# A two-layer hybrid diffusion trunk on one core: more room for row tasks, a second buffer of squares, and half of one pair's weight splits on VectorE

## The chip, the cores and the metric

The kernel runs on one core of one Trainium2 chip. The core has TensorE (PE in the profile; PEld is its weight load), VectorE (DVE), ScalarE (ACT), GpSimd (POOL) and SyncE (SP), which issues the transfers. The metric is the device time of one execution in microseconds; a kernel's time is the median of its runs.

## What is computed

One inference step over 640 tokens (128 context tokens and 512 latent tokens) of width 2048, through two layers. Each layer has the same frame; the mixers differ:

```python
m = silu(cond) @ ada_w + ada_b                     # shift, scale, gate: context and latent rows
x = rms_norm(h) * (1 + scale) + shift
parts = split(x @ w_in)                            # branches, and one gate path of width 2048
y = concat(mixer_1(parts), mixer_2(parts)) * silu(gate_path)
h = h + gate * (y @ w_out)
# layer 0: windowed attention with a sink || gated linear attention
# layer 1: 2-D neighbourhood attention   || spatial-gating MLP
...
out = rms_norm(h, g_final)                         # also the new caches and states
```

Everything is float32. What is large are the matrix products with w_in and w_out, and the reading of the `ada` weights, which are wanted for two conditioning rows only.

## The kernel before

**Tiles.** The width of 2048 is 16 tiles of 128; the 640 tokens are two halves of 320 (`HT`), so that a product's result of 128 x 320 fills a bank. A float32 product is made of three passes of rounded factors: the high part of the operand with the high and with the low part of the weight, and the low part of the operand with the high part of the weight. The high part (`whi`, `acth`) is a copy by ScalarE; the low part (`wlo`, `actl`) is raw minus high and is made by GpSimd, in some places by VectorE. All recorded operations of the engines stand in the profile as line L214, matmuls as L397, transposes as L402, and the loading of ScalarE's table for exponential and logarithm as L528.

**Order.** A planner in the kernel sets the order at build time. It keeps a cost table and a clock for each engine (`pace.t`: "v" VectorE, "a" ScalarE, "g" GpSimd, "t" TensorE), and while the matmuls are written down one after the other, `tick` (L482) advances other tasks between them: generators that wait for flags (`wait`), for a tile (`until`) or for an engine not to be too far ahead (`calm`). At run time each engine goes through its own list in order.

**Rows.** `self.low` is the lowest task, `ada_task`: the products of the `ada` weights with the two conditioning rows, one 512-wide row of sums after another on VectorE (`adas<-adas,bank,part`, then a read of the accumulator). While product buffers exist, some rows go to GpSimd (`prod<-adas,mixrow`) and ScalarE sums them into `psum`. Such a step is written only while VectorE's planned end is no later than `now + room` (L496). `rooms` (L417) has three values: 0 for most of the kernel, 1.5 from `open_g0` on (the last gates of layer 0 and its output projection), and 0.9 in the softmax stage of layer 0, set in `spill_y`. At the end of the rows for layer 1 the four sums of `psum` are added to `part` on VectorE, and the scale `A` and the flag `ada_1` follow.

**Around the change.** The program goes from the last gate chunks of layer 0 to its output projection (`out_proj`), then to layer 1's first products. Before a product with w_out or w_in, `handover` rewrites the 16 tiles into `acth` and `actl` while the last chunks of the stage before still run: handover "y0" ahead of the output projection, "x1" ahead of layer 1. Chunks come in pairs with a folded product (`pair("k", ...)`); the pair ahead of x1 is `fo0`, the first pair of layer 1 is x1.

**Squares.** `out_evac` evicts a chunk of the output projection: VectorE makes `Y` from the bank, the gate G and the old x; then `ssq_add` squares it on ScalarE into `self.sq` (`arena<-Y`) and adds it on GpSimd to `self.ssq` (`arena<-arena`). All squares of layer 0 use one buffer, `rest[:, 364 : 364 + CUT]`. After the last chunk `rstd1` multiplies `ssq` with ones and makes the reciprocal root with logarithm and exponential on ScalarE, which is where L528 loads its table. Slots A to H, R and Y0 to Y7 are pieces of the arena and of the row buffers; `clear` waits until their earlier use is over. R is `rest[:, 0:T]`.

**Splits.** `wstart` makes the list of weight splits. `self.both` holds the chunks whose `wlo` alternates between VectorE and GpSimd; before the change that is only the pair of kind "h" at the end of the kernel.

## Time and profile before

| | us |
|---|---|
| median of 3 runs | 2116.16 (2115.36 to 2120.01) |
| the profiled execution | 2115.62 |
| its span on the core | 2113.5 |

| engine | busy us | share of the span |
|---|---|---|
| TensorE matmul | 2055.7 | 97% |
| VectorE | 1309.8 | 62% |
| GpSimd | 1287.8 | 61% |
| ScalarE | 1071.7 | 51% |

The profile is one execution, taken on the chip. Its page gives each engine's busy time; windows give the same for any stretch with the granted clock of TensorE; the timeline lists instructions by start, with the idle time ahead of them in brackets and what ended it. Where every engine is at half load and TensorE at 97%, a busy share says little: what is to be read are the few places where TensorE waits.

### The profile page before, as it was taken

How to read it: one execution, taken by the hardware profiler on the slowest of the kernel's cores; microseconds unless marked ns; L12 is line 12 of the kernel's file. 1: busy time of each engine (PE TensorE's matmuls, PEld its weight loads, DVE VectorE, ACT ScalarE, POOL GpSimd, SP SyncE). 2: the span in 40 equal slices, each digit the busy share in tenths (PEclk: the TensorE clock that was granted, in tenths of full speed). 3: DMA queues.
4: the chain of work that ended last, by engine and by line, in shares of the span. 5: the costliest groups of instructions: out<-in, count | busy, mean ns of one | idle time of the engine just before them, and what ended most of it. 6: DMA issues, size and time to landing. Idle time of an engine off the chain costs nothing. (4 is left out here: it accounts for less than half of the span.)

```text
span 2113.5 us, 40246 instructions
## 1 busy us (share of the span) xinstructions
PE 2055.7 (97%) x14345; PEld 2002.0 (95%) x14345; DVE 1309.8 (62%) x3047; ACT 1071.7 (51%) x2471; POOL 1287.8 (61%) x1089
## 2 busy tenths in 40 slices
PE   7999999999999999999989999999999999999996
PEld 6899999999999999999989999999999999999996
DVE  4756686666555554888666878787454544455334
ACT  5645565454566665543464434444444554454443
POOL 4666575445545444797575666555555577768883
PEclk9999999999999999999999999999999999999998
DMA  9966343336454444566733444444222344363426
GB/s 362 389 224 199 121 147 112 119 110 199 139 198 155 141 149 136 174 229 222 235 109 121 137 161 150 135 156 146 91 82 94 101 137 130 121 221 123 132 93 239
DMA packets 192841, 340.18 MB, mean 161 GB/s; under 512 B 20896, under 2 KB 70144, under 8 KB 192640
## 3 DMA queue, kind: packets, MB, share of 16 engines
q1 hardware_dynamic: 191296, 336.45, 47.8%
q8 instruction: 112, 1.84, 0.3%
q10 hardware_dynamic: 1344, 1.17, 0.2%
q14 instruction: 89, 0.73, 0.1%
HBM read 303.03 MB, written 31.88 MB: 158 GB/s over the span
## 5 line engine op out<-in xcount | busy, mean ns | idle before, releaser
L397 PE MATMUL bank<-acth,whi 128*128 128x320 f32 (+3 forms) x3320 | 1022.0, 319 | 12.1 <-DVE arena L214 2.4
L397 PE MATMUL bank<-actl,whi 128*128 128x320 f32 (+3 forms) x3320 | 994.3, 310 | 4.0 <-POOL actl L214 3.4
L397 PE MATMUL bank<-acth,wlo 128*128 128x320 f32 (+3 forms) x3320 | 994.6, 311 | 3.2 <-POOL wlo L214 3.2
L214 POOL TENSOR_TENSOR wlo<-wraw,whi 128x512 fp32r<-128x512 f32 (+1 forms) x450 | 569.8, 1278 | 402.4 <-ACT whi L214 312.1
L397 PEld LDWEIGHTS bank<-acth,whi 128*128 128x128 f32 (+1 forms) x3320 | 617.7, 189 | 21.9 <-ACT bc L214 3.5
L397 PEld LDWEIGHTS bank<-actl,whi 128*128 128x128 f32 (+1 forms) x3320 | 617.6, 189 | 7.4 <-POOL actl L214 4.4
L397 PEld LDWEIGHTS bank<-acth,wlo 128*128 128x128 f32 (+1 forms) x3320 | 617.8, 189 | 4.6 <-POOL wlo L214 4.6
L214 POOL TENSOR_TENSOR wlo<-rs,whi 128x384 fp32r<-128x384 f32 x370 | 407.0, 1119 | 184.9 <-ACT whi L214 142.7
L214 ACT ACTIVATE whi<-wraw 128x512 fp32r<-128x512 f32 (+1 forms) x456 | 260.5, 587 | 93.2 <-PE bank L397 66.2
L397 PE MATMUL bank<-eh,whi 128*128 128x322 f32 (+1 forms) x666 | 208.9, 314 | 0.0
L397 PE MATMUL bank<-eh,wlo 128*128 128x322 f32 (+1 forms) x666 | 206.7, 310 | 1.5 <-POOL wlo L214 1.5
L214 ACT ACTIVATE whi<-rs 128x384 fp32r<-128x384 f32 x370 | 182.7, 516 | 49.3 <-PE bank L397 43.1
L397 PE MATMUL bank<-el,whi 128*128 128x322 f32 (+1 forms) x666 | 206.7, 310 | 0.0
L214 DVE TENSOR_TENSOR wraw<-rs 128x768 f32<-128x768 f32 x74 | 96.6, 1305 | 122.2 <-DMA rs<-w_odd 50.4
L214 DVE CUSTOM_DVE_ANT_0 adas<-adas,bank,partg 128x256 bf16<-128x256 f32 (+1 forms) x290 | 156.2, 538 | 12.0 <-DMA adas<-ada_g 4.7
L214 POOL TENSOR_TENSOR prod<-adas,mixrow 128x512 f32<-128x512 f32 x85 | 110.6, 1310 | 71.3 <-ACT prod L214 48.3
L214 ACT ACTIVATE arena<-arena,bc 128x512 f32<-128x512 f32 (+4 forms) x211 | 106.4, 527 | 81.2 <-DVE arena L214 78.4
L397 PEld LDWEIGHTS bank<-eh,wlo 128*128 128x128 f32 x666 | 125.5, 188 | 2.8 <-POOL wlo L214 2.8
L397 PEld LDWEIGHTS bank<-el,whi 128*128 128x128 f32 x666 | 125.8, 189 | 0.0
L397 PEld LDWEIGHTS bank<-eh,whi 128*128 128x128 f32 x666 | 125.5, 188 | 0.0
L214 DVE CUSTOM_DVE_ANT_0 adas<-adas,bank,part 128x512 bf16<-128x512 f32 x151 | 112.3, 744 | 9.5 <-DMA adas<-ada 6.4
L214 DVE TENSOR_TENSOR bank<-bank,sums 128x320 f32<-128x320 f32 (+1 forms) x148 | 71.1, 494 | 71.7 <-PE bank L397 55.9
(216 smaller groups left out, 2445.2 us busy)
## 6 DMA issues: line engine op xcount, KB each, us to landing
wraw<-w_even SPq DMA_DIRECT2D x176, 256.0 KB, 3.3
adas<-ada_g SPq DMA_DIRECT2D x128, 256.0 KB, 3.6
adas<-ada SPq DMA_DIRECT2D x128, 256.0 KB, 3.7
rs<-w_odd SPq DMA_DIRECT2D x50, 384.0 KB, 3.2
wraw<-w_odd SPq DMA_DIRECT2D x74, 256.0 KB, 3.6
wraw<-w_out SPq DMA_DIRECT2D x60, 256.0 KB, 3.7
rs<-w_odd SPq DMA_DIRECT2D x50, 256.0 KB, 3.8
Y<-ada SPq DMA_DIRECT2D x24, 512.0 KB, 7.5
```

The costliest lines, as they stand in the source:

```text
L214: return f(*args, **kw)
L397: self.nc.tensor.matmul(out, lhsT, rhs, start=start, stop=stop, **kw)
```

## The change

- `rooms[2]` is 1.5 in place of 0.9: in the softmax stage rows are written while VectorE is up to 1.5 us ahead of the plan's clock.
- The squares of layer 0's output use two buffers in turn, the second in slot R, which `clear` now waits for; the last two chunks (`n >= KT - 2`) add their squares on VectorE in place of GpSimd.
- `self.both` also holds the first pair of layer 1 (x1): half of its `wlo` go to VectorE.
- The table load has a method of its own, `tables`, and is called ahead of `need("ada_1")`, so before the last pair of the output projection and not at `rstd1`.
- Between the four additions for layer 1 the task gives way for 2.0 us of the plan's clock.

```diff
@@ -414,7 +414,7 @@
     lags0, room0, rows_at, pace0, NRAW, NRING = (0.2,) * 5, 1.2, 20.0, 0.4, 5, 6
     dve = (4, 5, 10, 11, 8, 9)
     lags2, cap2 = (8.0, 6.0, 4.0, 1.0, 0.4), 2.0
-    rooms, calms, lags = (0.0, 1.5, 0.9), (3.0, 3.0), (3.0, 3.0, 2.0, 1.0, 0.4)
+    rooms, calms, lags = (0.0, 1.5, 1.5), (3.0, 3.0), (3.0, 3.0, 2.0, 1.0, 0.4)
 
     def dma(self, out, in_):
 
@@ -521,13 +521,16 @@
             yield WAIT
 
 
+    def tables(self):
+        if self.actset != "e":
+            self.tc.nc.scalar.preload_act_table_set(ACTSET)
+            self.actset = "e"
+            self.pace.table()
+
     def act(self, out, in_, f, **kw):
         nc = self.nc
         if f in (AF.Exp, AF.Ln):
-            if self.actset != "e":
-                self.tc.nc.scalar.preload_act_table_set(ACTSET)
-                self.actset = "e"
-                self.pace.table()
+            self.tables()
         elif f == AF.Silu:
             if self.actset != "s":
                 self.pace.table()
@@ -554,7 +557,7 @@
                     if j % 4 == 0:
                         unit(c, j)
         last = None
-        self.both = {c for kind, x in acts if kind == "h" for c in x[:2]}
+        self.both = {c for kind, x in acts if kind == "h" or kind == "k" and x[3] == "x1" for c in x[:2]}
         seven = {c for kind, x in acts if kind == "s" for c in x}
         for kind, x in acts:
             if kind == "c" and x >= FIRST:
@@ -1196,14 +1199,14 @@
         nc.vector.scalar_tensor_tensor(self.rstd[:, c], t[:, :HT], 1.5, self.rstd[:, c], ALU.add, ALU.mult)
         yield
 
-    def ssq_add(self, ssq, x, k, sq, c=slice(0, T)):
+    def ssq_add(self, ssq, x, k, sq, c=slice(0, T), eng=None):
         nc = self.nc
         if k == 0:
             nc.scalar.activation(ssq[:, c], x[:, c], AF.Square)
         else:
             sq = sq[:, : c.stop - c.start]
             nc.scalar.activation(sq, x[:, c], AF.Square)
-            nc.gpsimd.tensor_tensor(ssq[:, c], ssq[:, c], sq, ALU.add)
+            (eng or nc.gpsimd).tensor_tensor(ssq[:, c], ssq[:, c], sq, ALU.add)
 
 
     def act_mod(self, l, k, x, t0, t1):
@@ -1287,6 +1290,8 @@
                     for q in range(4):
                         acc = self.part[name][:, :, 1]
                         nc.vector.tensor_tensor(acc, acc, self.psum[:, q, 0 : acc.shape[1]], ALU.add)
+                        if name == "1":
+                            yield 2.0
                 last[0][1]()
                 self.flags.add("ada_" + last[0][0])
                 self.top = {"1": 7, "g1": 8}.get(last[0][0], self.top)
@@ -1931,14 +1936,15 @@
             if l == 1 and f == KT - 1:
                 nc.scalar.activation(self.sq[:, : c.stop - c.start], y[:, c], AF.Square)
             else:
-                self.ssq_add(self.ssq, y, f, self.sq, c)
+                eng = nc.vector if l == 0 and n >= KT - 2 else nc.gpsimd
+                self.ssq_add(self.ssq, y, f, self.sq if self.cut == CUT else self.sqs.next(), c, eng)
 
         def evac(pa, pb):
             G, at = self.G[l], self.cut
             y = self.Y[:, n % NY, :]
             if pa is not None:
                 if n < NY:
-                    self.clear(f"Y{n}", "C")
+                    self.clear(f"Y{n}", "C", "R")
                 x = box["x"]
                 nc.vector.scalar_tensor_tensor(
                     y[:, 0:NCTX], pa[:, 0:NCTX], G[:, f, 0:1], x[:, 0:NCTX], ALU.mult, ALU.add
@@ -2337,7 +2343,7 @@
             S = self.slots
             L["gz"] = self.xr = Ring([S["A"], S["B"]])
             L["ms"] = [S["A"][:, :CUT], S["B"][:, :CUT]]
-            self.ssq, self.sq = S["C"], rest[:, 364 : 364 + CUT]
+            self.ssq, self.sq, self.sqs = S["C"], rest[:, 364 : 364 + CUT], Ring([rest[:, 0:HT], rest[:, 364 : 364 + HT]])
             x = self.ar[:, 4 * T : 4 * T + 1024]
             self.wsT, self.gb = (x[:, 512 * i : 512 * i + 512].rearrange("p (a b) -> p a b", b=128) for i in range(2))
             L["vr"] = Ring([S[n] for n in "ABCD"])
@@ -2393,6 +2399,7 @@
         k = acts.pop()
         at1 = {f: f"Y{i % NY}" for i, f in enumerate(OUT0) if i >= NY}
         do(lambda: self.spawn(shift1()))
+        do(self.tables)
         do(lambda: self.need("ada_1"))
         do(
             lambda: self.handover(
```

What this does to the order of instructions, at the three places with the largest shifts. Over the whole kernel nine rows go from VectorE to GpSimd, four weight splits from GpSimd to VectorE, and four additions of squares too; TensorE has the same instructions, in another order in the softmax stage and in the first products of layer 1.

ScalarE's list at the handover to layer 0's output projection (about 840 us in the profile). `bc` are the shift columns of a gate chunk, the three rows behind them its SiLU; `acth` is the rewriting of the mixer's output, `whi` the weight split. Before:

```order
L214 ACTIVATE whi<-wraw 128x512 x2
L214 ACTIVATE acth<-arena_8110 128x640 x3
L214 ACTIVATE whi<-wraw 128x512
L214 ACTIVATE acth<-arena_8110 128x640
L214 ACTIVATE bc_8347<-bank_67 128x2
L214 ACTIVATE arena_8110<-arena_8110,bc_8347 128x128
L214 ACTIVATE arena_8110<-arena_8110,bc_8347 128x192
L214 ACTIVATE arena_8110<-arena_8110,bc_8347 128x320
```

Here the weight split and the fourth `acth` stand ahead of `bc`. After the change:

```order
L214 ACTIVATE whi<-wraw 128x512 x2
L214 ACTIVATE acth<-arena_8163 128x640 x3
L214 ACTIVATE bc_8399<-bank_67 128x2
L214 ACTIVATE arena_8163<-arena_8163,bc_8399 128x128
L214 ACTIVATE arena_8163<-arena_8163,bc_8399 128x192
L214 ACTIVATE arena_8163<-arena_8163,bc_8399 128x320
L214 ACTIVATE acth<-arena_8163 128x640
```

The two weight splits stand further ahead, and the fourth `acth` behind the first gate.

VectorE's list at the end of the rows of layer 1 (`ISA` is a row's sum, and the read of its accumulator). Before, at about 1020 us, between evictions of the output projection:

```order
L214 ISA adas,part_111<-adas,bank_73,part_111 128x512
L214 ISA part_111 128x1
L214 ISA adas,part_111<-adas,bank_74,part_111 128x512
L214 ISA part_111 128x1
L214 TENSOR_TENSOR part_111<-part_111,psum 128x32 x4
L214 TENSOR_TENSOR A_97<-part_111,b_94 128x16
L214 TENSOR_TENSOR A_97<-A_97,small 128x16
L214 TENSOR_TENSOR A_97<-part_111,b_94 128x16
L214 TENSOR_TENSOR A_97<-A_97,small 128x16
L214 TENSOR_TENSOR sums_8106<-sums_8106,bank_71 128x320
L214 TENSOR_TENSOR bank_70<-bank_70,sums_8106 128x320
L214 SCALAR_TENSOR_TENSOR Y<-bank_70,G_98,arena_8110 128x320
```

The four additions and the making of `A` stand in one piece, ahead of the eviction of bank_71 and bank_70 (`sums`). After the change the same point of the list is reached some 45 us earlier in the program:

```order
L214 ISA adas,part_111<-adas,bank_74,part_111 128x512
L214 ISA part_111 128x1
L214 TENSOR_TENSOR part_111<-part_111,psum 128x32 x3
L214 TENSOR_TENSOR wraw<-rs_8158 128x768
L214 TENSOR_TENSOR bank_71<-bank_71,sums_8159 128x320
L214 TENSOR_TENSOR bank_69<-bank_69,sums_8159 128x320
L214 SCALAR_TENSOR_TENSOR Y<-bank_69,G_98,arena_8163 128x128
L214 SCALAR_TENSOR_TENSOR Y<-bank_69,G_98,arena_8163 128x192
L214 SCALAR_TENSOR_TENSOR Y<-bank_71,G_98,arena_8163 128x320
L214 TENSOR_TENSOR part_111<-part_111,psum 128x32
L214 TENSOR_TENSOR rs_8158<-wraw,rs_8158 128x768
L214 TENSOR_TENSOR A_97<-part_111,b_94 128x16
```

Three additions still stand together; the fourth comes behind five steps of a chunk's eviction, and `A` behind it.

VectorE's list at the last eviction of the output projection (about 1063 us). The banks 67, 70, 68 and 69 hold the four results of the pair fo0. Before:

```order
L214 TENSOR_SCALAR arena_8110<-arena_8110,A_97 128x128
L214 TENSOR_SCALAR arena_8110<-arena_8110,A_97 128x512
L214 SCALAR_TENSOR_TENSOR Y<-bank_67,G_98,arena_8110 128x128
L214 SCALAR_TENSOR_TENSOR Y<-bank_67,G_98,arena_8110 128x192
L214 SCALAR_TENSOR_TENSOR Y<-bank_70,G_98,arena_8110 128x320
L214 SCALAR_TENSOR_TENSOR Y<-bank_68,G_98,arena_8110 128x128
L214 SCALAR_TENSOR_TENSOR Y<-bank_68,G_98,arena_8110 128x192
L214 SCALAR_TENSOR_TENSOR Y<-bank_69,G_98,arena_8110 128x320
L214 TENSOR_TENSOR el_8104<-bank_71,eh_8103 128x320
```

The six steps that make `Y` follow each other without a break. After the change:

```order
L214 TENSOR_SCALAR adas<-adas,A_97 128x128
L214 SCALAR_TENSOR_TENSOR Y<-bank_67,G_98,arena_8163 128x128
L214 SCALAR_TENSOR_TENSOR Y<-bank_67,G_98,arena_8163 128x192
L214 TENSOR_TENSOR arena_8163<-arena_8163 128x320
L214 SCALAR_TENSOR_TENSOR Y<-bank_70,G_98,arena_8163 128x320
L214 TENSOR_TENSOR arena_8163<-arena_8163 128x320
L214 TENSOR_TENSOR wlo<-wraw,whi 128x512
L214 SCALAR_TENSOR_TENSOR Y<-bank_68,G_98,arena_8163 128x128
L214 SCALAR_TENSOR_TENSOR Y<-bank_68,G_98,arena_8163 128x192
L214 TENSOR_TENSOR arena_8163<-arena_8163 128x320
L214 SCALAR_TENSOR_TENSOR Y<-bank_69,G_98,arena_8163 128x320
L214 TENSOR_TENSOR arena_8163<-arena_8163 128x320
```

Behind each of the four results stands the addition of its square (`arena<-arena`), which needs ScalarE's square of that `Y`, and among them a weight split. On ScalarE the load of the table stands behind the squares of the chunk before fo0, about 35 us earlier than it did.

## The prediction

> **What bounds the kernel now.** I read the page first, then the stages in windows, then the gaps in TensorE's timeline. The page:
>
> ```profile
> span 2113.5 us, 40246 instructions
> PE 2055.7 (97%) x14345; PEld 2002.0 (95%) x14345; DVE 1309.8 (62%) x3047; ACT 1071.7 (51%) x2471; POOL 1287.8 (61%) x1089
> ```
>
> TensorE is busy for 97% and its work is the same after the change (the order has the same number of TensorE instructions), so only its idle or half-clocked time can change. The profiled execution took 2115.6 us, the span and 2.1 us around it, 0.5 under the median of the runs (2116.2). Everything below is a sum against 2115.6. The windows (start:end, length, then busy time and count of PE, PEld, DVE, ACT, POOL, the granted clock, DMA share, GB/s) show where that time lies:
>
> ```profile
> 612.00:812.00 200.00, 198.78 (x1319) 190.79 (x1318) 113.90 (x335) 134.61 (x349) 98.56 (x76) 1.00 0.45 144
> 845.00:850.00 5.00, 4.92 (x23) 4.92 (x24) 2.72 (x7) 2.67 (x6) 1.04 (x2) 0.66 0.37 118
> 880.00:980.00 100.00, 98.36 (x664) 97.09 (x663) 88.10 (x196) 42.76 (x97) 86.07 (x79) 1.00 0.66 222
> 980.00:1030.00 50.00, 47.15 (x316) 46.16 (x316) 43.40 (x90) 17.87 (x41) 36.56 (x36) 1.00 0.60 187
> 1065.00:1070.00 5.00, 5.00 (x36) 5.00 (x35) 2.64 (x6) 0.95 (x2) 3.83 (x4) 1.00 0.78 284
> 1080.00:1085.00 5.00, 5.00 (x23) 4.84 (x24) 5.00 (x7) 3.05 (x6) 3.87 (x3) 0.66 0.20 70
> 2010.00:2060.00 50.00, 50.00 (x342) 50.00 (x342) 19.68 (x30) 20.68 (x45) 41.79 (x40) 1.00 0.30 98
> ```
>
> Three things. The softmax stage (612 to 812) has 1.2 us of idle time in 200: nothing to win, something to lose. The end of layer 0's output projection (980 to 1030) passes 316 matmuls where the undisturbed end of the kernel passes 342 of the same size in as long: 26 x 50/342 = 3.8 us are lost there. And in two 5 us windows, around 847 and 1082, the clock column falls to 0.66 and 23 matmuls pass where 36 do at full clock: 13 x 5/36 = 1.8 us each, of which I take 1.7. The timeline of TensorE (start, duration, form, then the idle time ahead and who ended it) names the waits in these places:
>
> ```profile
> 606.13 0.33 PE L402 MATMUL bank<-ident,arena 128*128 128x128 f32 x1 [1.75 <-ACT arena L214]
> 680.56 0.33 PE L402 MATMUL bank<-ident,arena 128*128 128x128 f32 x1 [1.22 <-ACT arena L214]
> 845.08 0.41 PE L397 MATMUL bank<-acth,whi 128*128 128x320 f32 x1 [1.86 <-DVE arena L214]
> 1015.47 0.41 PE L397 MATMUL bank<-eh,wlo 128*128 128x320 f32 x1 [0.49 <-POOL wlo L214]
> 1021.82 0.41 PE L397 MATMUL bank<-acth,wlo 128*128 128x320 f32 x1 [0.79 <-POOL wlo L214]
> 1026.90 0.41 PE L397 MATMUL bank<-acth,whi 128*128 128x320 f32 x1 [1.58 <-DVE sums L214]
> 1060.85 0.41 PE L397 MATMUL bank<-acth,wlo 128*128 128x320 f32 x1 [1.23 <-POOL wlo L214]
> 1077.36 0.41 PE L397 MATMUL bank<-acth,whi 128*128 128x322 f32 x1 [1.19 <-ACT acth L214]
> 1079.82 0.42 PE L397 MATMUL bank<-actl,whi 128*128 128x322 f32 x1 [1.90 <-POOL actl L214]
> ```
>
> The clock falls right behind the waits of 1.86 and 1.90 us and not behind those of 1.75 and 1.58. So a wait in this kernel seems to cost its own length, and 1.7 us more once it is nearer to 1.9 than to 1.75.
>
> **A. Rows in the softmax stage: +1.5 us.** With the room at 1.5 us instead of 0.9, the order has 14 more rows of layer 1 on VectorE and 8 more products on GpSimd by the end of that stage. VectorE's rows come in pairs at 24 places instead of 14, in singles at 21 instead of 24. What one costs:
>
> ```profile
> L214 DVE CUSTOM_DVE_ANT_0 adas<-adas,bank,part 128x512 bf16<-128x512 f32 x151 | 112.3, 744 | 9.5 <-DMA adas<-ada 6.4
> L214 DVE DVE_READ_ACCUMULATOR2_ANT part<- 128x1 f32 x215 | 17.7, 82 | 0.0
> L214 POOL TENSOR_TENSOR prod<-adas,mixrow 128x512 f32<-128x512 f32 x85 | 110.6, 1310 | 71.3 <-ACT prod L214 48.3
> ```
>
> A row holds VectorE for 0.744 + 0.082 = 0.83 us, so the stage gets 11.6 us more on VectorE and 8 x 1.31 = 10.5 us on GpSimd. Both fit (113.9 and 98.6 busy of 200 in the window). What can hurt is a row that stands ahead of a softmax operation for which the transposes wait, as at 606 and 680. Ten more pairs are ten chances of 0.83 us, 8.3 us if each stalled; the window shows that TensorE nearly always has other matmuls, so I take one in five or six, +1.5. Bounds: -1 (rows out of the way of one of the waits) and +5 (six stalls).
>
> **B. The handover to layer 0's output projection, about 840: -2.9 us.** The wait of 1.86 us at 845.08, for an eviction by VectorE, ends a chain that begins on ScalarE:
>
> ```profile
> 840.98 0.61 ACT L214 ACTIVATE whi<-wraw 128x512 fp32r<-128x512 f32 x1
> 841.50 0.72 ACT L214 ACTIVATE acth<-arena 128x640 fp32r<-128x640 f32 x1
> 842.13 0.15 ACT L214 ACTIVATE bc<-bank 128x2 f32<-128x2 f32 x1
> 843.09 1.53 DVE L214 TENSOR_TENSOR Y<-Y,arena 128x320 f32<-128x320 f32 x1 [2.29 <-ACT arena L214]
> ```
>
> VectorE stood idle for 2.29 us until ScalarE had made the gate (SiLU of the chunk and its shift columns, `bc`), then multiplied by it, and only then evicted the bank. Before the change one weight split (0.61) and one operand split (0.72) stand ahead of `bc`; in the new order the weight split is issued before and the operand split behind the first gate. That starts the gate up to 1.3 us sooner; since the operand of that split is also wanted, I take 1.1. The wait falls to 0.76 us and the half clock with it: -1.1 - 1.7 = -2.8, and 0.1 for the following small waits: -2.9. Bounds: 0 (the operand split becomes the late one) and -3.6 (wait and half clock both gone).
>
> **C. The end of layer 0's output projection: -3.4 us.** Here the rows of layer 1 end before, and then four additions and their followers run in one piece:
>
> ```profile
> 1020.77 4.23 DVE L214 TENSOR_TENSOR part<-part,psum 128x32 f32<-128x32 f32 x4
> 1024.92 1.02 DVE L214 TENSOR_TENSOR A<-part,b 128x16 f32<-128x16 f32 x1
> ```
>
> 4.23 and then about 1 us stand in front of the bank's eviction, and TensorE waits 1.58 us for it (1026.90, "DVE sums"). In the new order the rows end some 45 us sooner (14 in the softmax stage, and 9 on GpSimd in all), the additions come between 975 and 990, three in one run and one further on, with a chunk's evictions between them, and the last 45 us of the projection have no rows, so that weight splits on GpSimd come on time. Of the 3.8 us lost in this window, the three waits quoted are 0.49 + 0.79 + 1.58 = 2.86; I take 3.4, most of the way to the pace of the kernel's end, because the small start-to-start losses go too. The same additions now lie within 880 to 980, where VectorE is busy for 88%: three of them, 3 x 1.06 us, can show a wait of their own there. Bounds: -1.6 (only the wait at 1026.90 goes, or the others come back earlier) and -3.8.
>
> **D. The start of layer 1's projections, 1060 to 1083: -4.9 us.** The waits at 1060.85, 1077.36 and 1079.82 and two behind them:
>
> ```profile
> 1063.57 1.12 DVE L214 SCALAR_TENSOR_TENSOR Y<-bank,G,arena 128x128 f32<-128x128 f32 x3
> ...
> 1066.30 0.86 POOL L214 TENSOR_TENSOR arena<-arena 128x320 f32<-128x320 f32 x1
> ...
> 1067.19 0.47 ACT L214 ACTIVATE arena<-Y 128x320 f32<-128x320 f32 x1 [2.41 <-POOL arena L214]
> ...
> 1072.78 1.28 ACT L528 ACT_TABLE_LOAD   x1
> ...
> 1072.77 5.50 POOL L214 TENSOR_TENSOR wlo<-wraw,whi 128x512 fp32r<-128x512 f32 x4
> 1078.23 3.06 POOL L214 TENSOR_TENSOR actl<-adas,acth 128x640 fp32r<-128x640 f32 x2
> ...
> 1075.14 0.51 DVE L214 SCALAR_TENSOR_TENSOR arena<-rstd 128x320 f32<-128x320 f32 x1 [7.50 <-ACT rstd L214]
> ...
> 1087.81 0.42 PE L397 MATMUL bank<-actl,whi 128*128 128x322 f32 x1 [0.28 <-POOL actl L214]
> ...
> 1090.64 0.41 PE L397 MATMUL bank<-actl,whi 128*128 128x322 f32 x1 [0.78 <-POOL actl L214]
> ```
>
> There are four squares (ScalarE) and four additions (GpSimd) on one buffer; each square waits for the addition before it (1067.19: 2.41 us). From 1066.30 on GpSimd is late with all: four additions of 0.87, an operand split, four weight splits (5.50), and only then the operand splits for which TensorE waits at 1079.82. Meanwhile VectorE idles for 7.50 us. The change takes the four additions (3.5 us) and four weight splits of 1.37 (5.5 us) from GpSimd to VectorE and the table load (1.28) out of ScalarE's chain to some 30 us earlier, behind the squares of the chunk before, where TensorE has other work; there I cost it at nothing (uncovered: 1.3). GpSimd would be ahead by 9.0 us at 1078, more than any wait here. So 1.23 + 1.19 + 1.90 + 0.28 + 0.78 = 5.4 us of waits can go, and the half clock's 1.7: 7.1.
>
> Against it stands a new order on VectorE: before, the evictions of the last two chunks ran in two unbroken runs (the three at 1063.57 in 1.12 us); now an addition stands behind each half, and waits for ScalarE's square. The price of such a wait is a square of 0.47 and an addition that, as between 320-wide operands at 1075.14 on the same engine, takes about 0.5, with 0.1 for the two handovers: 1.1 us. The pair's first matmuls want two of the four banks (the folded product holds the fifth), its second chunk the other two, and in each pair of banks the second is freed 1.1 us later than now: 2 x 1.1 = 2.2. The four weight splits on VectorE have their price from the few that it makes now:
>
> ```profile
> L214 DVE TENSOR_TENSOR wlo<-wraw,whi x6: 693/878/1555, 2061.0 to 2095.2; 128x512 fp32r<-128x512 f32 x6
> ```
>
> 4 x 0.88 (1.56 at worst) fit in the 7.5 us of idle time. -7.1 + 2.2 = -4.9. Bounds: -7.1 (the banks' delay hidden by the fold's other matmuls) and -1 (the new waits long enough to halve the clock again, and the split on VectorE late behind the additions).
>
> The other edits add no instruction: the second square buffer lies in slot R, which was read earlier for the last time, and clearing it in the order moves none. **Sum:** 1.5 - 2.9 - 3.4 - 4.9 = -9.7 us, 2115.6 - 9.7 = **2105.9 us**.
>
> [...]
>
> **Rivals.** *1. The half clock stays.* 1.75 gave none and 1.86 did: two cases on either side are a thin base, and it might hang on where a wait falls in some fixed window and not on its length. Then other waits halve the clock in place of these, and the kernel wins only the idle time: -9.7 + 3.4, 2109.3. For it: the steps last equally long wherever they begin. Chance 0.13.
>
> *2. VectorE's order eats the gain at the pair.* The additions wait in order for squares, the squares stand on ScalarE behind weight splits of 0.61 us, and the banks come free 2 x 2.2 us late; one such wait is over 1.86 us and halves the clock. D is then -7.1 + 4.4 + 1.7 = -1.0 and the kernel at 2109.8; with the additions of C stalling the busy window before 980 by 1 us too, 2110.8. For it: nothing is queued on VectorE that could go ahead. Against: the wait of 7.50 us leaves it much room. Chance 0.17.
>
> *3. Slower: rows in front of the softmax.* If each of the 24 pairs makes a block's transposes wait for its second row, that is 24 x 0.83 = 19.8 us in a stage that has lost 1.2, and B to D bring 11.2: 2115.6 + 19.8 - 11.2 = 2124.2. It decides from 11.2 / 0.83 = 14 pairs on, and is told from no change from 19 on. For it: the waits at 606 and 680 end with the softmax's own data. Against: TensorE has other matmuls to put between, 198.8 busy in 200, and before the change singles and pairs left almost no trace. Chance 0.12.
>
> **How the numbers follow.** My forecast has 0.58. About 0.2% (4.2 us) is what a measurement of this kernel can tell from no change, so "faster" begins at 2111.4 below the profiled execution. Forecast, rival 1 and most of rival 2 lie beyond it, less the cases in which A comes out at its +5 or C and D at their small ends: 0.72 faster. Same 0.16: the rest of rival 2 and of the forecast, and rival 3 with 14 to 19 pairs or somewhat fewer. Slower 0.12 by rival 3. The range: down to all gains at their ends, -1 - 3.6 - 3.8 - 7.1 = -15.5, 2100.1; up to 2115.6, no change at all, which holds both smaller rivals and B to D at their small ends (0, -1.6, -1) with A at +2.6, and leaves out rival 3 and little else.
>
> **What would show it.** A: TensorE's busy time from 612 to 812 stays at 198 or more in 200, and no wait for "ACT arena" is new there. B: the wait at the handover is under 1 us and the clock column stays at 1.00. C: the last 50 us of layer 0's output projection pass some 340 matmuls, with no "DVE sums" wait over 1 us, none either where the additions now stand. D: no wait over 1.8 us and no 0.66 within 40 us of the first pair; ScalarE's squares no longer wait for GpSimd; TensorE's new waits there name VectorE. I am wrong in mechanism if the softmax stage loses more than 5 us, or if the pair's waits for GpSimd are still there.

## The result, and the profile after

| | before | changed |
|---|---|---|
| median of 8 runs each, us | 2117.92 (2114.92 to 2120.37) | 2111.08 (2108.44 to 2113.52) |
| ratio, with its 95% interval | | 0.9967 (0.9956 to 0.9978) |
| profiled execution, us | 2115.62 | 2113.52 |

The change takes 6.8 us off (4.7 to 9.3). The profiled execution of the changed kernel happens to be the slowest of its eight, so the two profiles differ by 2 us only. Its page:

```profile
span 2111.7 us, 40271 instructions
PE 2056.5 (97%) x14345; PEld 2004.6 (95%) x14345; DVE 1304.9 (62%) x3034; ACT 1079.9 (51%) x2493; POOL 1297.6 (61%) x1090
```

TensorE has 14345 recorded matmuls in both, in the same order but for some stretches. So the start of the n-th matmul after, counted from the first matmul, can be set against that of the n-th before, and the difference between two such points is what the stretch between them won or lost. I take numbers 4400, 5800, 6400, 7220 and 7700. The first four stand outside the reordered stretches; 7700 stands a few matmuls before the end of the last one, and number 7720 in its place moves D by 0.2 us at most:

| stretch (us of the profile before) | forecast | measured |
|---|---|---|
| up to 594, where nothing is changed | 0 | +6.4 |
| softmax stage, 594 to 808 (A) | +1.5 | -2.4 |
| handover, 808 to 903 (B) | -2.9 | +1.2 |
| output projection to its end, 903 to 1029 (C) | -3.4 | -5.1 |
| layer 1's first pair, 1029 to 1109 (D) | -4.9 | -0.6 |
| A to D | -9.7 | -6.9 |
| behind 1109, to the last matmul | 0 | -1.4 |

The first and last rows are scatter between executions: eleven more profiles below start with +0.3 to +5.2 and differ behind 1109 by -1.8 to +3.1, with the same order there. The four stretches together give the change of the medians; but only C comes near the size that I gave it, and lies past its bound, and two terms have the other sign. The windows that answer to those before:

```profile
612.00:812.00 200.00, 199.67 (x1336) 192.73 (x1337) 127.28 (x378) 142.68 (x378) 110.20 (x85) 1.00 0.50 162
880.00:980.00 100.00, 99.03 (x672) 98.28 (x671) 93.10 (x207) 41.71 (x95) 86.83 (x79) 1.00 0.68 220
980.00:1030.00 50.00, 50.00 (x343) 50.00 (x342) 23.28 (x37) 20.46 (x45) 44.82 (x41) 1.00 0.44 143
```

The end of the projection runs at full pace, 343 matmuls where 316 passed. TensorE's waits from the timeline:

```profile
612.25 0.33 PE L402 MATMUL bank<-ident,arena 128*128 128x128 f32 x1 [0.78 <-ACT arena L214]
847.78 0.41 PE L397 MATMUL bank<-acth,whi 128*128 128x320 f32 x1 [0.93 <-ACT bc L214]
850.27 0.64 PE L397 MATMUL bank<-acth,whi 128*128 128x320 f32 x1 [2.08 <-DVE arena L214]
972.55 0.41 PE L397 MATMUL bank<-acth,wlo 128*128 128x320 f32 x1 [0.38 <-POOL wlo L214]
1065.83 0.42 PE L397 MATMUL bank<-acth,whi 128*128 128x320 f32 x1 [2.19 <-DVE Y L214]
1069.72 0.41 PE L397 MATMUL bank<-acth,whi 128*128 128x320 f32 x1 [0.95 <-DVE Y L214]
1086.93 0.42 PE L397 MATMUL bank<-acth,whi 128*128 128x322 f32 x1 [0.90 <-ACT acth L214]
1088.56 0.47 PE L397 MATMUL bank<-actl,whi 128*128 128x322 f32 x1 [1.06 <-POOL actl L214]
```

At the handover 1.86 has become 0.93 + 2.08. At the first pair the waits for GpSimd have shrunk, and two new ones for VectorE's `Y`, 3.1 us together, stand in their place: rival 2. What remains open from these two profiles: which edit brought each, and why the handover became worse.

### The profile page after: what moved, and what is told of

Same layout as the page of the kernel before. It is cut to its first block, busy times and chain, and to the rows that moved or that the text cites. A ratio compares the mean times of both kernels' runs of the same rounds, so it can differ in the third digit from the quotient of the medians.

```text
span 2111.7 us, 40271 instructions
## 1 busy us (share of the span) xinstructions
PE 2056.5 (97%) x14345; PEld 2004.6 (95%) x14345; DVE 1304.9 (62%) x3034; ACT 1079.9 (51%) x2493; POOL 1297.6 (61%) x1090
## 5 line engine op out<-in xcount | busy, mean ns | idle before, releaser
L214 POOL TENSOR_TENSOR prod<-adas,mixrow 128x512 f32<-128x512 f32 x94 | 123.1, 1319 | 84.2 <-ACT prod L214 58.6
L214 DVE CUSTOM_DVE_ANT_0 adas<-adas,bank,part 128x512 bf16<-128x512 f32 x142 | 105.6, 744 | 5.6 <-DMA adas<-ada 2.6
```

Of the source, the lines that this page charges most:

```text
L214: return f(*args, **kw)
```

## The experiments

Each run was profiled and timed; the table gives the four stretches against the profile before, their sum, the median and the ratio to the runs of before on the same chip. A stretch of one profile is one draw: kernels with the same order in a stretch differ there by up to 3.0 us (A of e4 and e8), mostly by a window of 3.41 us at a granted clock of 0.50, so 1.7 us, that falls in or out (last section). The profile before is one of the faster executions of its kernel (2115.62, where the medians of its runs in the later rounds are 2118 to 2119), so most sums here are 1.5 to 4.5 us smaller than what the medians gain (e1's is 2.8 larger).

| kernel | A | B | C | D | sum | median us | ratio (95%) |
|---|---|---|---|---|---|---|---|
| changed | -2.4 | +1.2 | -5.1 | -0.6 | -6.9 | 2111.08 | 0.9967 (0.9956-0.9978) |
| e1_rooms | -2.1 | +1.2 | -4.3 | -0.6 | -5.8 | 2116.01 | 0.9987 (0.9975-0.9999) |
| e2_room09 | -0.2 | +0.2 | -5.3 | +0.2 | -5.0 | 2109.53 | 0.9959 (0.9944-0.9974) |
| e3_pool_adds | -2.2 | +1.3 | -5.3 | -6.1 | -12.3 | 2104.42 | 0.9933 (0.9918-0.9948) |
| e4_no_both | +0.4 | +1.3 | -4.4 | -2.1 | -4.7 | 2112.05 | 0.9966 (0.9955-0.9978) |
| e5_buffers_only | -0.3 | -1.2 | -1.4 | -2.3 | -5.2 | 2111.39 | 0.9962 (0.9948-0.9975) |
| e7_late_adds | -2.0 | +1.5 | -4.7 | -4.4 | -9.6 | 2106.90 | 0.9940 (0.9927-0.9953) |
| e8_copies_held | -2.6 | -2.0 | -2.6 | -0.6 | -7.8 | 2108.81 | 0.9954 (0.9941-0.9967) |
| e9_pool_adds_held | -1.8 | -2.2 | -3.0 | -5.5 | -12.4 | 2102.64 | 0.9928 (0.9914-0.9943) |
| e10_spacing_only | +0.5 | -1.7 | -1.3 | +1.2 | -1.3 | 2116.84 | 0.9990 (0.9980-1.0000) |
| e11_best_no_tables | -1.3 | -0.5 | -4.4 | -3.8 | -10.0 | 2105.96 | 0.9943 (0.9928-0.9959) |
| e12_best_no_both | -1.7 | -2.0 | -2.9 | -1.4 | -8.0 | 2106.92 | 0.9944 (0.9929-0.9959) |

**The room, alone and taken back.** e1 is the kernel before with this line, e2 the changed kernel without it:

```diff
-    rooms, calms, lags = (0.0, 1.5, 0.9), (3.0, 3.0), (3.0, 3.0, 2.0, 1.0, 0.4)
+    rooms, calms, lags = (0.0, 1.5, 1.5), (3.0, 3.0), (3.0, 3.0, 2.0, 1.0, 0.4)
```

> The kernel before with only the softmax stage's room at 1.5. Told apart: whether the room alone carries what changed from 600 to 1030 us (softmax stage -2.4, handover to the output projection +1.2, end of the output projection -5.0 against before, each read at equal places of TensorE's list), or whether the spacing of the four additions does part of the last. Theory (room alone): -2.4, +1.2 and -4.5 to -5.0, nothing at layer 1's first pair, in all -5.7 to -6.2 us, with the two waits of 0.93 and 2.08 at the handover as in the changed kernel. Rival (the spacing counts): a wait for the sums of over 1 us is still there where the four additions now stand, the end of the output projection gives -3.5 or less, in all -4.7 or less.

> The changed kernel with the room back at 0.9, all else as changed. Theory (room carries the middle, the rest only layer 1's first pair): softmax stage and handover as before (the 1.86 wait is back, the 0.93 and 2.08 are gone), the end of the output projection within 1 us of before except that the spaced additions may take the 1.58 wait away (-1 to -1.6), the first pair -0.6 with the two waits for VectorE's Y of about 2.2 and 0.95: in all -0.6 to -2.2. Rival (the parts need each other): the pair's gain or the handover's loss differs by more than 1.5 us from these.

A and B belong to the room: e1 has them (B with waits of 0.37 and 2.40), e2 does not. In A the nine profiles at 1.5 have a mean of -1.7, the four at 0.9 one of 0.0; the one that stands out is e4 (+0.4), with a wait of 2.11 us for transposes at 610 and a window at half clock behind it. C belongs to both, which neither theory had: the room alone gives -4.3, the rest alone -5.3 where -1 to -1.6 was expected, both together -5.1. In time the rest alone gains 4.1 permille, all of it 3.3 with overlapping intervals, the room alone 1.3: on top of the rest, the room brings nothing that these runs can show. At the first pair e2 has the first of the two waits expected for `Y` (2.19) but not the second, and two windows at half clock (0.50, one of them at 1064.12), where the changed kernel has one (0.50, at 1088.76): +0.2 in place of -0.6.

**What makes up C.** e5 is the kernel before with the second buffer only, e10 the kernel before with the spacing only:

```diff
-                self.ssq_add(self.ssq, y, f, self.sq, c)
+                self.ssq_add(self.ssq, y, f, self.sq if self.cut == CUT else self.sqs.next(), c)
...
-                    self.clear(f"Y{n}", "C")
+                    self.clear(f"Y{n}", "C", "R")
...
-            self.ssq, self.sq = S["C"], rest[:, 364 : 364 + CUT]
+            self.ssq, self.sq, self.sqs = S["C"], rest[:, 364 : 364 + CUT], Ring([rest[:, 0:HT], rest[:, 364 : 364 + HT]])
```

> The kernel before with only the second buffer of squares; all additions stay on GpSimd, room 0.9, no other edit. Theory (the one buffer makes ScalarE wait for GpSimd's addition before each second square, about 1 us, and the weight splits behind it come late): the four waits for GpSimd's splits between 962 and 1022 (0.28, 0.79, 0.49, 0.79) go, -2.0 to -2.4 there; the 1.58 for the sums stays; at layer 1's first pair the chain of squares and additions shortens by 1 to 2 us and the waits of 1.19 and 1.90 shrink: in all -2.5 to -6 us. Rival (these waits come from the rows on VectorE, which end at 1020 here as before): the four waits stay, nothing up to 1030, at most -1 in all.

```diff
                         nc.vector.tensor_tensor(acc, acc, self.psum[:, q, 0 : acc.shape[1]], ALU.add)
+                        if name == "1":
+                            yield 2.0
```

> The kernel before with only the 2.0 us of giving way between the four additions for layer 1. Theory (the additions in one piece hold up the eviction that TensorE waits for at 1026.9): that wait falls from 1.58 to under 0.9 us, nothing else up to 1030: -0.7 to -1.6 there, and at the first pair 0 within 1.8 us, the cost of one window at half clock, which may fall in or out. Rival (the wait comes from the late splits of the chunk before, not from the additions): it stays over 1.2 us, within 0.4 of before.

TensorE's waits in the stretch from 930 to 1030 (us in total, times, longest), first before:

```profile
PE bank L397 <- POOL wlo L214: 2.3, 4, 0.8
PE bank L397 <- DVE sums L214: 1.6, 1, 1.6
```

with two buffers only:

```profile
PE bank L397 <- DVE sums L214: 2.9, 1, 2.9
```

with the spacing only:

```profile
PE bank L397 <- POOL wlo L214: 2.9, 4, 0.8
```

and with the room only:

```profile
PE bank L397 <- POOL wlo L214: 0.8, 1, 0.8
```

The buffer takes the four waits for splits, the spacing the one for the sums, each as its theory had it and nothing of the other. How the buffer does it is seen on ScalarE. Before, the second square of a chunk waits for GpSimd to add the first, and the weight splits stand behind it:

```profile
957.65 0.47 ACT L214 ACTIVATE arena<-Y 128x320 f32<-128x320 f32 x1 [5.49 <-DVE Y L214]
959.11 0.47 ACT L214 ACTIVATE arena<-Y 128x320 f32<-128x320 f32 x1 [0.99 <-POOL arena L214]
959.48 0.42 ACT L214 ACTIVATE sums<-bank 128x320 f32<-128x320 f32 x1
959.80 0.93 ACT L214 ACTIVATE whi<-wraw 128x384 fp32r<-128x384 f32 x2
```

With two buffers both squares run back to back, and the splits begin 1.16 us behind the start of the first square and not 2.15:

```profile
957.64 0.93 ACT L214 ACTIVATE arena<-Y 128x320 f32<-128x320 f32 x2 [4.78 <-DVE Y L214]
958.48 0.42 ACT L214 ACTIVATE sums<-bank 128x320 f32<-128x320 f32 x1
958.80 0.93 ACT L214 ACTIVATE whi<-wraw 128x384 fp32r<-128x384 f32 x2
```

In e5 TensorE comes to the sums sooner, and its wait there grows from 1.6 to 2.9, which takes 1.3 back: that is why C is only -1.4 in it, short of the -2.0 to -2.4 expected, while the whole is clearly faster. By time the second buffer alone (0.9962) gains as much as the whole change (0.9967): no other single edit tried on the kernel before comes near it (room 0.9987, spacing 0.9990).

**The first pair.** e3 takes the additions of the last two chunks back to GpSimd, with both buffers; e4 takes the pair's splits back; e7 leaves the additions on VectorE, but puts them behind all evictions:

```diff
-                eng = nc.vector if l == 0 and n >= KT - 2 else nc.gpsimd
+                eng = nc.gpsimd
```

> The changed kernel with the last two chunks' squares added on GpSimd again (two buffers stay). Theory (the additions standing in VectorE's list ahead of the next eviction are what TensorE waits for at the first pair): the two waits for VectorE's Y, 2.19 and 0.95, go, and GpSimd is 4 x 0.87 = 3.5 us later with its splits, so that part comes back as waits for GpSimd: at the pair 0 to -2.5 us against the changed kernel. Rival (the weight split on VectorE, or the eviction itself, delays the banks): waits for VectorE's Y of over 1.5 us together remain, and the pair costs as much or up to 2 us more.

```diff
-        self.both = {c for kind, x in acts if kind == "h" or kind == "k" and x[3] == "x1" for c in x[:2]}
+        self.both = {c for kind, x in acts if kind == "h" for c in x[:2]}
```

> The changed kernel without the first pair in the set whose splits alternate: all its low parts on GpSimd. Theory: the first wait for VectorE's Y stays at 1.5 to 2.3 (an addition, not a split, stands ahead of that eviction), the second shrinks by up to the split's 0.69; GpSimd gets four splits of 1.4 back, so that the waits for its operand splits grow by 0.5 to 2.5 us: 0 to +2 against the changed kernel. Rival (the split on VectorE is what delays the banks): both waits for VectorE's Y go and the pair is 1.5 to 3 us faster.

```diff
+                if l == 0 and n >= KT - 2:
+                    sq = box["x"][:, c]
+                    nc.scalar.activation(sq, y[:, c], AF.Square)
+                    self.tail.append((self.ssq[:, c], sq))
...
             yield from self.wait(*(f"evac{c}" for c in cs))
+            for o, sq in self.tail:
+                nc.vector.tensor_tensor(o, o, sq, ALU.add)
```

> The changed kernel with the four additions of the last two chunks still on VectorE, but behind all six evictions (the squares go to the old x's tiles, which are free by then, so that none waits for a buffer). Theory (the additions' place in VectorE's list is what costs, not the engine): no wait for VectorE's Y over 0.5 us at the first pair, which comes out at -4 to -6.5 us against before, like the run with the additions on GpSimd. Rival (VectorE itself is too full there): other waits for VectorE take their place, and the pair is at -2 or worse.

VectorE's timeline in the changed kernel shows the price of an addition ahead of an eviction:

```profile
1063.84 1.47 DVE L214 TENSOR_TENSOR arena<-arena 128x320 f32<-128x320 f32 x1 [0.73 <-ACT arena L214]
1065.24 0.54 DVE L214 SCALAR_TENSOR_TENSOR Y<-bank,G,arena 128x320 f32<-128x320 f32 x1
1066.38 0.49 DVE L214 TENSOR_TENSOR arena<-arena 128x320 f32<-128x320 f32 x1 [0.61 <-ACT arena L214]
```

The first costs 0.73 of waiting for the square and 1.47 of its own, 2.2 us, and TensorE's wait at 1065.83 is 2.19 for the eviction at 1065.24. e7 runs the six evictions in two unbroken pieces, and the additions come after:

```profile
1062.76 1.12 DVE L214 SCALAR_TENSOR_TENSOR Y<-bank,G,arena 128x128 f32<-128x128 f32 x3
...
1065.76 1.12 DVE L214 SCALAR_TENSOR_TENSOR Y<-bank,G,arena 128x128 f32<-128x128 f32 x3
...
1067.60 2.79 DVE L214 TENSOR_TENSOR arena<-arena 128x320 f32<-128x320 f32 x4
```

In e7 and e3 no wait for `Y` is left; from 1030 to 1110 e7 waits as in the first row, e3 as in the second:

```profile
PE bank L397 <- POOL actl L214: 1.8, 2, 1.0
```

```profile
PE bank L397 <- POOL actl L214: 1.4, 2, 1.0
```

So it is the additions' place in the list, not VectorE as such, that costs: D is -4.4 and -6.1 against -0.6. (What makes e7 1.7 us slower than e3 there, beyond 0.4 us of waits, is open.) My expectation for e3 (0 to -2.5 against the changed kernel) was too small: I added the 3.5 us to GpSimd's work as if it had none to spare. In the changed kernel it stands idle at this place:

```profile
1070.83 1.29 POOL L214 TENSOR_TENSOR wlo<-wraw,whi 128x512 fp32r<-128x512 f32 x1 [5.86 <-ACT whi L214]
```

In e3 the four additions fill this gap. The squares do wait for them again, even with two buffers, but TensorE does not see it:

```profile
1060.27 0.47 ACT L214 ACTIVATE arena<-Y 128x320 f32<-128x320 f32 x1 [1.67 <-POOL arena L214]
```

And 1.7 of the 5.5 us is a half clock window (0.50 for 3.41 us from 1088.76 on in the changed kernel) that fell out: the mean granted clock of the profiled execution is 0.996, the changed kernel's 0.994. e4's theory held for the waits for `Y` (2.20 and 0.30), but the stretch came out 1.4 faster than the changed kernel, not 0 to 2 slower; it has no half clock window there, the changed kernel one, and without that the two are level.

**The handover.** Orders and traces give a chain for B. ScalarE at the end of layer 0's attention, before:

```profile
813.38 0.17 ACT L214 ACTIVATE bc<-bank 128x2 f32<-128x2 f32 x1
```

and in the changed kernel, in which everything stands 3.8 us later at this point:

```profile
817.15 1.11 ACT L214 ACTIVATE bank<-adas 128x512 f32<-128x512 f32 x2
818.19 0.62 ACT L214 ACTIVATE mixrow<-adas 128x512 f32<-128x512 f32 x1
818.72 0.16 ACT L214 ACTIVATE bc<-bank 128x2 f32<-128x2 f32 x1
```

The rows have run so far ahead that the last quarter's conditioning rows are due: three copies that stand ahead of the stage's last gate. SyncE's queue shows what comes of it, before and after:

```profile
817.72 1.75 SPq L431 DMA_DIRECT2D arena<-yT_dram  x4
...
835.01 1.33 SPq L431 DMA_DIRECT2D arena<-yT_dram  x3
```

```profile
823.05 1.75 SPq L431 DMA_DIRECT2D arena<-yT_dram  x4
...
840.91 0.85 SPq L431 DMA_DIRECT2D arena<-yT_dram  x2
```

The loads of the mixer's output go out 823.05 - 3.8 - 817.72 = 1.5 us late, the second group 2.1 us, and the operand splits for which `bc` waits in ScalarE's list follow. In the changed kernel the last of them waits for its load, and `bc` comes right behind it:

```profile
846.93 0.74 ACT L214 ACTIVATE acth<-arena 128x640 fp32r<-128x640 f32 x1 [0.35 <-DMA arena<-yT_dram]
847.57 0.15 ACT L214 ACTIVATE bc<-bank 128x2 f32<-128x2 f32 x1
```

(The copies into `bank` are 512 wide: a bank holds more than a product's 320 columns, which take a bank but do not fill it.) e8 holds the copies until the product buffers are closed, e9 holds them in the kernel of e3:

```diff
             if len(job) == 2:
+                while "ya7" in self.flags and self.prods:
+                    yield 0.4
```

> The changed kernel with one hold: the last quarter's conditioning rows, three copies by ScalarE that stand ahead of the last gate of layer 0's attention, wait until the product buffers are closed, and the last quarter's rows then all run on VectorE. Theory (these copies, 1.8 us on ScalarE, make the last gate, the loads of the mixer's output and so the handover late): the loads start 1.5 us sooner, the handover costs 1.2 to 1.5 us less than in the changed kernel, as before the change; the rows end 10 to 15 us later, still ahead of the end of the output projection (+-0.5 there): in all -1 to -1.5 against the changed kernel. Rival (the changed order of splits and operand splits on ScalarE costs the handover): it stays within 0.4 us of the changed kernel's.

> The changed kernel with the additions on GpSimd again and the copies held: both suspected losses taken back. Theory: the sum of the two, softmax stage -2.2, handover 0, end of the output projection -5.2, first pair -6.0 against before, in all -13 to -14 us, 1 to 1.5 below the run with the additions on GpSimd alone. Rival (the parts meet: rows that end later than without the hold stand in the projection's end): the end of the projection gives 1 us or more less, and the sum is no better than without the hold.

With the hold B falls from +1.2 to -2.0 (e8) and from +1.3 to -2.2 (e9), and in e8 the loads go out at 816.30, which with the 1.4 us that e8 is ahead there is the place that they have before. So what the hold takes away is the cause. One thing limits the reading: with the hold the planner also puts the splits ahead of `bc` back into the order before, so that the runs alone do not separate the copies from e8's rival, the order of the splits; what speaks for the copies is the chain of late loads above. e11 and e12 below have the hold too and the same order up to this place: -0.5 (with a wait of 1.91 us that the other three do not have) and -2.0. All four with the hold lie below all five without it (+1.2 to +1.5), by 3.0 us in the mean, twice what e8 expected, because the half clock goes too (0.50 for 3.41 us from 849.83 on in the changed kernel; from 600 to 1110 the granted clock is 1.00 in e9 and 0.99 in the changed kernel). The price is the rival of e9. The numbers of rows on VectorE and GpSimd do not change (142 and 94), but in TensorE's list the rows of the last quarter begin 31 matmuls (4.6 us) and end 11 matmuls (1.7 us) later, and C gives 2.4 us less in both (e11 0.9 less than e3, e12 2.4); e8 expected 0.5 at most. By the stretches e9 equals e3; by time it is 0.5 permille faster, which the intervals do not separate. e9 has the lowest time of all, 0.9928 of before (0.9914 to 0.9943), some 8 us below the changed kernel.

**Table and split, in the kernel of e9.** Each without one edit: e11 without the call of `tables`, e12 with `both` as before the change.

```diff
-        do(self.tables)
```

> The run with the additions on GpSimd and the copies held, without the early load of the table. Theory (the load stands between the last square and the reciprocal root, for which the splits of the first pair wait): 1.28 us later there, of which TensorE sees 0.3 to 1.3 as waits for an operand split at the first pair. Rival (hidden by other matmuls): the pair within 0.3 us.

> The run with the additions on GpSimd and the copies held, with all low parts of the first pair's weights on GpSimd. Theory (GpSimd has the four additions of 0.87 and gets four splits of 1.4 back, 5.5 us in a stretch where it is the late one): the waits for GpSimd at the first pair grow by 1 to 4 us. Rival (GpSimd has room again once squares no longer wait for it): within 0.5 us, as the kernel with the additions on VectorE lost nothing without this edit.

Both edits pay in D: it loses 1.7 us without the early table and 4.1 without the split (theory 0.3 to 1.3, and 1 to 4), with no window at half clock there in any of the three (mean granted clock 0.997 in e9, 0.996 in e11, 0.997 in e12). The medians are 3.3 and 4.3 us higher, but the intervals overlap a little, so time alone does not show it. In e11 the waits are not where its theory had them: two for weight splits, 1.24 and 1.58 us, and none of that size for an operand split. In e12 the waits for GpSimd from 1030 to 1110 are

```profile
PE bank L397 <- POOL actl L214: 2.3, 4, 0.8
PE bank L397 <- POOL wlo L214: 1.8, 2, 1.1
```

4.1 us in place of 1.4. In the changed kernel this gain of the split could not be seen (e4), probably because VectorE's additions held up the pair first; that is argued, not shown.

## Why the prediction was right or wrong

The direction and the range held: 6.8 us were won, 9.7 forecast from the profiled execution. That the sum came near is in good part luck, because errors of both signs met. Of the signs that the prediction named, those for A and C came; those for B (a wait under 1 us at full clock) and D (no wait over 1.8 us, no half clock) did not.

- **A, wrong in sign.** "What can hurt is a row that stands ahead of a softmax operation": 14 more rows stand there, and the stretch is some 2 us faster. The wait for transposes near 680 is 1.21 and 1.22 us in the three runs at 0.9 (e2, e5, e10) and in none at 1.5. In TensorE's new order these transposes stand behind more matmuls (the first is number 4955 and not 4943). That the planner puts them there because it counts the rows as VectorE's time is argued, not shown. The step that failed: I took TensorE's order for given, although the order showed that it moves there.
- **B, wrong in sign.** The term rested on ScalarE's list just ahead of `bc`, and the list did change so. But I read the eight lines around `bc`, and the three copies stand some 25 instructions further up; they make everything in these lines late. Also, the 1.86 with its half clock (0.50 from 845.59 on) was one execution's draw: runs with the order before had 2.05 with half clock (e2), 1.29 (e5) and 0.86 (e10) without. The four profiles with the order before have a mean of -0.7 in B (0, +0.2, -1.2, -1.7), the five with the new order one of +1.3: the change costs 2.0 us there.
- **C, right in sign, past its bound, the cause only one of two.** I gave it to rows that end sooner, with the additions between other steps. That is enough alone (e1, -4.3, with the last row at 976 and not at 1020) but not needed (e2, -5.3, with the last row at 1021.5): the four waits for splits have the single buffer as their cause (e5) and the wait for the sums the unspaced additions (e10); what the room takes and what these two take is largely the same time. The two waits at 962 and 969, 1.1 us of the same kind, were missing from the term, which is what put the result past its bound of -3.8.
- **D, the mechanism named, its size far off.** The new waits behind VectorE's additions were put at 2.2 us and measured 3.1. An addition was priced at 0.5, from the 0.51 at 1075.14; the one at 1063.84, with GpSimd at work, took 1.47, the one at 1066.38, with GpSimd idle, 0.49. And of the 7.1 us that I took to go, 2.0 us of waits and the half clock stayed, at 1087. Rival 2 gave D -1.0; -0.6 was measured.
- **The half clock** was removed in B and in D in my sum, 1.7 us each; it is in the changed profile at both places (0.50 from 849.83 and from 1088.76 on), so rival 1 was right too, with the cause that it named: where a wait falls in a fixed window. In these profiles that window is 3.413 us long (last section).
- **The slower rival** fell: TensorE's busy time in the softmax stage rose to 199.7 of 200.

## What to carry to other kernels

A single buffer between two engines cost here more than the wait of its writer (0.99 us at 959.11): the weight splits behind the writer in its list came late, and TensorE waited 2.3 us for them from 930 to 1030, not at all with two buffers. So give it a second buffer before moving work to another engine. When work is moved to an engine that also frees banks, look at what it waits for and put it behind the evictions (D was -4.4 so in e7, and -0.6 in the changed kernel). Where one edit lets a low-priority stream run ahead, look for the rarer steps of that stream (here three copies a quarter) and where they come to stand; and do not price a stretch from one execution's clock.

## What was not expected of the hardware

**In these profiles the half clock began on a grid of 3.413 us.** From 20 to 2085 us the profile before has the granted clock at 0.50 from 60.52, 845.59 and 1081.11 on, for 3.413 us each; the second and third begin 785.07 and 1020.59 us behind the first, which is 230 and 299 times 3.413. The changed kernel's has it from 61.35, 115.97, 849.83 and 1088.76 on, 16, 231 and 301 times 3.413 behind the first; that at 115.97 lasts 6.827 us, two windows, the others 3.413. I summed TensorE's idle time over the windows of that grid in both profiles. The six windows with the most (1.86, 1.90 and 1.94 us before, 1.97, 2.34 and 2.57 after) were followed by one at half clock; of the six between 1.3 and 1.8 us one was (1.65), and five were not (1.39, 1.40, 1.42, 1.64 and 1.75); of the ten between 1.0 and 1.3 none was, and of all those below 1.0 one (0.60, itself at half clock). Three pairs of grid windows in the changed kernel, each a wait and what follows:

```profile
846.42:849.83 3.41, 0.84 (x4) 0.35 (x3) 1.30 (x2) 1.70 (x5) 2.81 (x2) 1.00 0.46 175
849.83:853.24 3.41, 2.97 (x11) 2.98 (x12) 1.76 (x4) 2.11 (x5) 1.55 (x1) 0.50 0.22 58
1061.46:1064.87 3.41, 2.19 (x15) 1.91 (x13) 2.68 (x4) 2.21 (x5) 3.41 (x3) 1.00 0.04 14
1064.87:1068.28 3.41, 2.45 (x16) 2.45 (x17) 2.64 (x6) 1.06 (x3) 0.10 (x1) 1.00 0.44 164
1085.35:1088.76 3.41, 1.44 (x8) 0.92 (x7) 3.10 (x9) 3.05 (x7) 1.84 (x3) 1.00 0.43 147
1088.76:1092.18 3.42, 3.42 (x14) 3.42 (x14) 2.71 (x5) 3.21 (x7) 2.01 (x2) 0.50 0.18 60
```

The wait of 2.19 us at 1065.83 is cut by the grid at 1064.87 (its two windows are idle for 1.22 and 0.96 us) and costs only itself, while two short ones of 0.90 and 1.06 fall in one window, idle for 1.97, and the next is at 0.50. In e2, with the grid elsewhere, the same wait of 2.19 falls almost whole into one window, idle for 2.06, and the next is at 0.50:

```profile
1060.71:1064.12 3.41, 1.35 (x9) 1.05 (x7) 2.68 (x5) 1.37 (x3) 2.67 (x3) 1.00 0.21 64
1064.12:1067.53 3.41, 3.28 (x12) 3.29 (x13) 2.21 (x6) 1.46 (x3) 0.00 (x0) 0.50 0.40 146
```

The grid's place differed from run to run (60.52 before, 61.35 after, from the span's start), and so did the places of the waits; the 1.7 us behind a long wait (half of 3.41) was a chance here and not a constant.

**An addition on VectorE took three times as long beside GpSimd.** The addition at 1063.84 took 1.47 us while GpSimd ran

```profile
1063.65 1.32 POOL L214 TENSOR_TENSOR actl<-adas,acth 128x640 fp32r<-128x640 f32 x1
```

until 1064.97; the next, of the same size and with GpSimd idle, took 0.49. The first ended at 1065.31, 0.34 us behind GpSimd's instruction. Whether it had waited for that instruction or had run beside it more slowly, the trace does not show.
